# Merge gates and branch projections with the activations held in the array instead of the weights

## The chip, the core and the metric

One core of a Trainium2 chip runs the whole program. The metric is device time in microseconds (us), the median of three runs. TensorE (PE) multiplies, VectorE (DVE) and ScalarE (ACT) do the elementwise work, GpSimd (POOL) a few tiny operations, and SyncE (SP) starts most transfers from memory; ACT starts the others.

## What is computed

One residual block on 256 tokens of 2048 channels: a SwiGLU network, token mixing by three parallel branches, a second SwiGLU network, each between normalizations. The change is in the merge of the branches:

```python
gates = jax.nn.sigmoid(h @ w_merge_gate[l] + b_merge_gate[l])     # 2048 -> 3 x 2048
g_fox, g_diff, g_mem = jnp.split(gates, 3, axis=-1)
merged = (g_fox * (y_fox @ w_branch_fox[l])                       # 1024 -> 2048
          + g_diff * (y_diff @ w_branch_diff[l])                  #  512 -> 2048
          + g_mem * (y_mem @ w_branch_mem[l]))                    #  512 -> 2048
x = x + rmsnorm(merged @ w_out[l], mix_post_g[l])
```

## The kernel before

All weights stream through once, about 430 MB in pieces of 512 KB. SP loads a piece (`raw`, L65, six buffers), ACT rounds it to float32r (`hi`, L90), DVE computes the remainder (`lo`, L91), and TensorE reads both (four buffers of `hi` and `lo`). `Stream.ahead` (L69) issues ACT's and DVE's work for the pieces to come, as far as the four buffers allow, so the work for the piece that is three further on waits until TensorE has finished the piece before the current one. Everything runs in the order in which it is written: each engine, and SP's queue of transfers, takes its instructions in program order.

A product is made of three float32r products, hi*hi, hi*lo and lo*hi, and there are two forms:

- `mm_a` (L203) holds a 128 x 128 block of weights in the array and moves the activations through it, which lie transposed (channels on the partitions): `hi` with 512 columns (256 tokens, their hi and lo parts side by side) and `lo` with 256 columns. The result has channels on the partitions and must be summed from the two halves of its bank (`lr_sum`, L415).
- `mm_b` (L226) holds a 128 x 128 block of activations (128 tokens) and moves 512 columns of weights: three matmuls of 512 columns for each of the two token halves `t`. The result has tokens on the partitions. A piece is 12 such matmuls. Both feed-forward networks, the value projection (428 columns) and the output projection work like this.

The merge (L938 to L974) uses `mm_a`. It loops over 16 groups `m` of 128 output channels: three gate products with `h2T` (the normalized activations) of 16 row blocks each, then 16 row blocks of branch products with `y_a` and `y_b`. For each `m`, ACT and DVE sum the halves, scale by the row `hrow`, add the bias and take the sigmoid (L967, bias by partition from `colt`), multiply, add, and split the sum into `mT` (L974), which is already laid out as the output projection wants it. In the first group the rest of the attention steps runs between the products (`fill`); what is left is drained at once (L947).

The feed-forward networks hold the activations too, and their results must be turned. They do this block by block of 512 channels: DVE transposes 32 x 32 squares (L442) into `fz`; 16 small transfers on SP's queue move the squares to their partitions (`regroup`, L444, into `fw`), issued after the second piece of the next block; after its seventh piece ACT and DVE split the result into the next input (`split`, L451). The tables of offsets `OFF` and `OFF_V` shift operands by 32 and 112 bytes from the start of a 256-byte line. `PostProj` (L359) is the output projection with its normalization; its gain rows `g_row` are 256 KB transfers on ACT's queue (L374), broadcast to all partitions.

Of the kernel before, what the change touches and what calls it, by code (L numbers as in the profile page):

```python
# [16 lines left out]
P = 128  # L17
# [16 lines left out]

C_G1, C_GM, C_GMEM, C_G2, C_B, C_HG = 0, 16, 32, 48, 64, 112
N_COLS = 113


class Stream:
# [29 lines left out]
    def ahead(self, most=8):  # L69

        for _ in range(most):
            if self.done == len(self.plan):
                break
            _, ap, extra = self.plan[self.done]
# [12 lines left out]
            hi, lo = (pool.tile([P, D // 2], F32R, tag=t + tag, name=t, align_bytes=LINE)[:, off:off + 2 * step]  # L87
                      .rearrange("p (k n) -> p k n", k=2)[:, :, 0:w] for t in ("hi", "lo"))
# [22 lines left out]
def tile_block(ctx, tc, x, mem, xt, memt, f1gu, f1d, wqk, wv, wmkv, wgate, wbr, wout, f2gu, f2d,  # L111
# [84 lines left out]

    def rows_of(pool, n, off, **kw):

        t = pool.tile([P, n * 2 * S + OFF], F32R, align_bytes=LINE, **kw)
        return t[:, off:off + n * 2 * S].rearrange("p (k s n) -> p k s n", k=n, s=2)  # L200
# [224 lines left out]
    def times_row(dst, row):  # L425
        if row is not None:
            nc.vector.tensor_tensor(out=dst, in0=dst, in1=row, op=ALU.mult)


    def ffn_up(idx, hT, rstd, setup, groups, inserts):  # L430
# [6 lines left out]
        def product(t, bank):  # L437
# [4 lines left out]
            nc.vector.transpose(out=state["z"][:, t], in_=sg[:, t])  # L442

        def regroup():  # L444

            for a in range(4):
                for q in range(4):
                    nc.sync.dma_start(out=state["w"][32 * q:32 * q + 32, :, a],
                                      in_=state["z"][32 * a:32 * a + 32, :, P * q:P * (q + 1)])

        def split(n):  # L451
            src = state["w"].rearrange("p t a (k i) -> p k (t a) i", k=4)
            hi, lo = (state["gh"][:, 4 * n:4 * n + 4, i].rearrange("p k (g i) -> p k g i", i=32) for i in range(2))
            for k in range(4):
                split_to(hi[:, k], lo[:, k], src[:, k])

# [5 lines left out]
        for n in range(FB):  # L462
# [12 lines left out]
            for t in range(2):  # L475
                product(t, bu[t])
            late = {1: regroup, 6: lambda n=n: split(n)}
        return state["gh"], late
# [6 lines left out]
    tp1 = g1_stack.enter_context(tc.tile_pool(name="ft1", bufs=1, side="left", reuse_waits="tile"))  # L485
    hT1 = rows_of(hpool, KT, 0, name="hT1")
    gh1 = rows_of(gp1, FT, 0, name="gh1")
    zeros = hpool.tile([P, 512], BF16, name="zeros")
# [49 lines left out]
    fgp = fg_stack.enter_context(tc.tile_pool(name="fg1", bufs=1, side="right", reuse_waits="tile"))  # L538
    mha = rows_of(yap, 8, 0, tag="y", name="mha")
    macc = [small.tile([P, 4], F32, name=f"macc{t}", bufs=1) for t in range(2)]  # L540
# [40 lines left out]
    h2T = rows_of(h2p, KT, OFF, tag="h", name="h2T")  # L581
    mhb = rows_of(ybp, 8, 0, tag="y", name="mhb")

# [170 lines left out]

    y_a = rows_of(yap, 8, OFF, tag="y", name="y_a")
    y_b = rows_of(ybp, 8, OFF, tag="y", name="y_b")

# [179 lines left out]

    mg_stack = ExitStack()  # L938
    mT = None
    for m in range(KT):  # L940
        zs = []
        for b in range(3):
            z = zp.tile([P, S], F32, tag="z", name="z", bufs=4)
            lr_sum(z, proj_a("gate", h2T), zp)
            times_row(z, hrow)
            zs.append(z)
        if m == 0:  # L947
            while fill.left():
                fill(drain=True)
            at_stack.close()  # L950
            mgp = mg_stack.enter_context(tc.tile_pool(name="mgp", bufs=1, side="left", reuse_waits="tile"))
            mT = rows_of(mgp, KT, 0, name="mT")
        bb = [new_bank("mm_br") for _ in range(3)]
        lims = [(0, 8), (8, 12), (12, 16)]
        for half in range(2):
            st.ahead()
            w, = st.take("br")
            for kk in range(8):
                k = half * 8 + kk
                i = 0 if k < 8 else (1 if k < 12 else 2)  # L960
                mm_a(bb[i], w, kk, (y_a, y_b)[half], kk, k == lims[i][0], k == lims[i][1] - 1)
            st.release()
        acc = None
        for b in range(3):
# [12 lines left out]


    h3T = rows_of(h2p, KT, 0, tag="h", name="h3T")
    fg_stack = ExitStack()  # L980
# [13 lines left out]

    post2.body()
    banks = post2.last(lag=7, first_done=first_half,
# [6 lines left out]
    def setup2():  # L1003
        fg_stack.close()
        mg_stack.close()
        yb_stack.close()
        gp = g2_stack.enter_context(tc.tile_pool(name="gh2", bufs=1, side="right", reuse_waits="tile"))
        tp = g2_stack.enter_context(tc.tile_pool(name="ft2", bufs=1, side="right", reuse_waits="tile"))
        return tp, rows_of(gp, FT, 0, name="gh2")

# [117 lines left out]
```

## Time and profile before

| | |
|---|---|
| median of three runs | 2212.86 us (2212.7 to 2212.89) |
| the profiled execution's own time | 2212.4 us |
| its span, first to last instruction | 2210.6 us |
| TensorE busy | 2200.3 us, 100% of the span, 10560 matmuls |
| DVE / ACT busy | 1284.7 us (58%) / 1035.8 us (47%) |
| mean granted TensorE clock | 0.999 |
| HBM read | 423.28 MB, 192 GB/s over the span |

A busy time is the time in which an engine has at least one instruction under way. Matmuls overlap each other, so a matmul's own duration (0.39 us for 512 columns) says little; what counts is the distance from one start to the next. The merge runs from about 1020 to 1393 us; the output projection follows until 1481 us.

### The profile page before, as it was taken

What the parts mean: (1) busy time and instruction counts of PE and PEld (TensorE: products, weight loads), DVE (VectorE), ACT (ScalarE), POOL (GpSimd) and SP (SyncE); (2) the same over time, 40 slices, a digit from 0 to 9 for tenths busy, and PEclk for the clock granted to TensorE, in tenths of its full rate; (3) what the DMA queues carried; (4) which work ended last, traced back from release to release, by engine and by line L of the source; (5) the groups of instructions that cost most, each with busy time, mean ns of one, the idle gap of its engine ahead of it and who ended that gap; (6) DMA issues with size and microseconds to landing.
All of it is one profiled execution on the core that took longest, in us unless ns stands there. A gap on an engine that the chain in (4) does not pass through costs nothing. (4 is left out here: it accounts for less than half of the span.)

```text
span 2210.6 us, 28170 instructions
## 1 busy us (share of the span) xinstructions
PE 2200.3 (100%) x10560; PEld 1865.1 (84%) x10560; DVE 1284.7 (58%) x1621; ACT 1035.8 (47%) x1452; POOL 13.5 (1%) x25
## 2 busy tenths in 40 slices
PE   9999999999999999999999999999999999999998
PEld 7888888888888899988888888888888888888887
DVE  6555555555444756766676767566555555554444
ACT  6444444444444644544555555456444444444442
POOL 0000000000000100000000000000000000000000
PEclk9999999999999999999999999999999999999999
DMA  8666656667766564544556565655766666666664
GB/s 307 198 226 208 201 186 231 204 211 231 224 207 198 172 192 150 181 161 150 185 189 191 186 194 186 207 182 173 236 204 199 198 220 205 189 217 213 197 198 131
DMA packets 150840, 438.78 MB, mean 198 GB/s; under 512 B 19632, under 2 KB 42544, under 8 KB 150704
## 3 DMA queue, kind: packets, MB, share of 16 engines
q1 hardware_dynamic: 145088, 427.96, 60.0%
q10 hardware_dynamic: 5616, 9.03, 1.3%
q8 instruction: 82, 1.34, 0.2%
q14 instruction: 54, 0.44, 0.1%
HBM read 423.28 MB, written 2.10 MB: 192 GB/s over the span
## 5 line engine op out<-in xcount | busy, mean ns | idle before, releaser
L91 DVE TENSOR_TENSOR lo<-raw,hi 128x1024 fp32r<-128x1024 f32 (+2 forms) x794 | 957.2, 1211 | 761.4 <-ACT hi L90 736.0
L90 ACT CAST hi<-raw 128x1024 fp32r<-128x1024 f32 (+2 forms) x794 | 818.9, 1037 | 846.2 <-PE mm_b L236 744.8
L207 PE MATMUL mm_a<-h2T,hi 128*128 128x512 f32 x1088 | 384.0, 395 | 0.0
L209 PE MATMUL mm_a<-h2T,lo 128*128 128x256 f32 x1088 | 306.8, 282 | 0.0
L234 PE MATMUL mm_b<-hi,hT 128*128 128x512 f32 x704 | 274.4, 390 | 0.5 <-ACT hi L90 0.5
L234 PE MATMUL mm_b<-hi,h3T 128*128 128x512 f32 x704 | 274.9, 390 | 0.0
L235 PE MATMUL mm_b<-lo,hT 128*128 128x512 f32 x704 | 274.5, 390 | 0.2 <-DVE lo L91 0.2
L236 PE MATMUL mm_b<-hi,h3T 128*128 128x512 f32 x704 | 274.4, 390 | 0.0
L236 PE MATMUL mm_b<-hi,hT 128*128 128x512 f32 x704 | 274.3, 390 | 0.0
L234 PE MATMUL mm_b<-hi,gh 128*128 128x512 f32 x704 | 274.3, 390 | 0.0
L235 PE MATMUL mm_b<-lo,h3T 128*128 128x512 f32 x704 | 274.3, 390 | 0.0
L236 PE MATMUL mm_b<-hi,gh 128*128 128x512 f32 x704 | 274.3, 390 | 0.0
L235 PE MATMUL mm_b<-lo,gh 128*128 128x512 f32 x704 | 274.3, 390 | 0.0
L207 PEld LDWEIGHTS mm_a<-h2T,hi 128*128 128x128 f32 x1088 | 204.5, 188 | 41.5
L209 PEld LDWEIGHTS mm_a<-h2T,lo 128*128 128x128 f32 x1088 | 206.3, 190 | 0.2
L235 PEld LDWEIGHTS mm_b<-lo,hT 128*128 128x128 f32 x704 | 132.2, 188 | 28.2 <-DVE lo L91 0.8
L234 PEld LDWEIGHTS mm_b<-hi,hT 128*128 128x128 f32 x704 | 132.2, 188 | 28.2 <-ACT hi L90 1.0
L236 PEld LDWEIGHTS mm_b<-hi,gh 128*128 128x128 f32 x704 | 132.2, 188 | 27.5
L236 PEld LDWEIGHTS mm_b<-hi,h3T 128*128 128x128 f32 x704 | 132.2, 188 | 27.3
L234 PEld LDWEIGHTS mm_b<-hi,gh 128*128 128x128 f32 x704 | 132.2, 188 | 27.3
L234 PEld LDWEIGHTS mm_b<-hi,h3T 128*128 128x128 f32 x704 | 132.3, 188 | 27.2
L235 PEld LDWEIGHTS mm_b<-lo,gh 128*128 128x128 f32 x704 | 132.2, 188 | 27.2
(208 smaller groups left out, 1940.8 us busy)
## 6 DMA issues: line engine op xcount, KB each, us to landing
raw<-in_f1gu SPq DMA_DIRECT2D x176, 512.0 KB, 5.0
raw<-in_f2gu SPq DMA_DIRECT2D x176, 512.0 KB, 4.8
raw<-in_wgate SPq DMA_DIRECT2D x96, 512.0 KB, 4.3
raw<-in_f1d SPq DMA_DIRECT2D x88, 512.0 KB, 4.5
raw<-in_f2d SPq DMA_DIRECT2D x88, 512.0 KB, 4.2
raw<-in_wv SPq DMA_DIRECT2D x48, 428.0 KB, 3.4
raw<-in_wqk SPq DMA_DIRECT2D x40, 512.0 KB, 4.4
raw<-in_wbr SPq DMA_DIRECT2D x32, 512.0 KB, 4.0
```

The source lines that it names most:

```text
L90: self.nc.scalar.copy(out=hi[:, i], in_=src[:, i])
L91: self.nc.vector.tensor_tensor(out=lo[:, i], in0=src[:, i], in1=hi[:, i].bitcast(F32), op=ALU.subtract)
L207: nc.tensor.matmul(bank, lhsT=hi[:, i, c], rhs=act[:, k].rearrange("p s n -> p (s n)"), start=start, stop=False)
L209: nc.tensor.matmul(bank[:, 0:S], lhsT=lo[:, i, c], rhs=act[:, k, 0], start=False, stop=stop)
L234: nc.tensor.matmul(o, lhsT=xh, rhs=wh, start=start and kk == 0, stop=False)
L235: nc.tensor.matmul(o, lhsT=xh, rhs=wl, start=False, stop=False)
L236: nc.tensor.matmul(o, lhsT=xl, rhs=wh, start=False, stop=stop and kk == 1)
```

## The change

The merge is written with `mm_b`. It loops over four blocks `n` of 512 output channels and, inside, over the three branches: 8 pieces of gate products into two banks, then 4 pieces (first branch) or 2 pieces (second and third) of branch products into two others. DVE scales a gate bank by the token's factor and adds the bias (L966); the bias is now a row of 512 channels, broadcast to all partitions by a 256 KB transfer on ACT's queue that stands in program order behind the gate's last piece (L963). ACT takes the sigmoid, DVE multiplies by the branch bank and adds up in `acc`. The first three blocks are turned as in the feed-forward networks: two DVE transposes, 16 small transfers after the second piece of the next block, the split after its seventh (`turned_block`, the old `regroup` and `split` moved out). The last block is turned by eight TensorE transposes after the second and third piece of the output projection. The weights of the first three blocks are reordered on the host, so that the turned squares come out in place. `y_a`, `y_b` lose their 32-byte shift, the gate weights get it; `h2T` keeps its own. A scratch size drops from 4096 to 2048 bytes, and `cols` loses its 48 bias columns.

```diff
-C_G1, C_GM, C_GMEM, C_G2, C_B, C_HG = 0, 16, 32, 48, 64, 112
+C_G1, C_GM, C_GMEM, C_G2, C_HG = 0, 16, 32, 48, 64
...
-            off, step = (OFF_V, NBS) if w == NB else (0, w)
+            off, step = (OFF_V, NBS) if w == NB else (OFF if name == "gate" else 0, w)
...
-    for m in range(KT):
-        for b in range(3):
-            st.add("gate", wgate[b * KT + m])
-        st.add("br", wbr[m])
+    for n in range(4):
+        for b, (lo, hi) in enumerate(((0, 2), (2, 3), (3, 4))):
+            for i in range(4):
+                st.add("gate", wgate[(4 * b + n) * 4 + i])
+            for i in range(lo, hi):
+                st.add("br", wbr[4 * n + i])
...
+    def turned_block(z, w, dst, n, at=(1, 6)):
+        def regroup():
+            for a in range(4):
+                for q in range(4):
+                    nc.sync.dma_start(out=w[32 * q:32 * q + 32, :, a],
+                                      in_=z[32 * a:32 * a + 32, :, P * q:P * (q + 1)])
+        def split():
+            src = w.rearrange("p t a (k i) -> p k (t a) i", k=4)
+            hi, lo = (dst[:, 4 * n:4 * n + 4, i].rearrange("p k (g i) -> p k g i", i=32) for i in range(2))
+            for k in range(4):
+                split_to(hi[:, k], lo[:, k], src[:, k])
+        return {at[0]: regroup, at[1]: split}
...
-    y_a = rows_of(yap, 8, OFF, tag="y", name="y_a")
-    y_b = rows_of(ybp, 8, OFF, tag="y", name="y_b")
+    y_a = rows_of(yap, 8, tag="y", name="y_a")
+    y_b = rows_of(ybp, 8, tag="y", name="y_b")
...
+    late = {}
+    for n in range(4):
         acc = None
-        for b in range(3):
-            g = zs[b]
-            c = C_B + b * KT + m
-            nc.scalar.activation(out=g, in_=g, func=AF.Sigmoid, bias=colt[:, c:c + 1])
-            br = zp.tile([P, S], F32, tag="br", name="br")
-            lr_sum(br, bb[b], zp)
-            nc.vector.tensor_tensor(out=g, in0=br, in1=g, op=ALU.mult)
-            if acc is not None:
-                nc.vector.tensor_tensor(out=g, in0=acc, in1=g, op=ALU.add)
-            acc = g
-        split_to(mT[:, m, 0], mT[:, m, 1], acc)
+        for b, y in enumerate((y_a, y_b[:, 0:4], y_b[:, 4:8])):
+            banks = proj_b("gate", h2T, KT, 512, steps=late)
+            late = {}
...
+            bias = mwp.tile([P, 512], F32, tag="bias", name="bias", bufs=2)
+            nc.scalar.dma_start(out=bias, in_=rows[3 + b:4 + b, 512 * n:512 * (n + 1)].partition_broadcast(P)[:, 0])
+            g = mwp.tile([P, 2, 512], F32, tag="g", name="g", bufs=2)
+            for t in range(2):
+                nc.vector.scalar_tensor_tensor(out=g[:, t], in0=banks[t], scalar=hr[t], in1=bias,
+                                               op0=ALU.mult, op1=ALU.add)
+                nc.scalar.activation(out=g[:, t], in_=g[:, t], func=AF.Sigmoid)
+            banks = proj_b("br", y, 8 if b == 0 else 4, 512)
...
+            for t in range(2):
+                o = acc[:, t] if b == 0 else g[:, t]
+                nc.vector.tensor_tensor(out=o, in0=banks[t], in1=g[:, t], op=ALU.mult)
+                if b:
+                    nc.vector.tensor_tensor(out=acc[:, t], in0=acc[:, t], in1=g[:, t], op=ALU.add)
+        if n < 3:
+            for t in range(2):
+                nc.vector.transpose(out=z[:, t], in_=acc[:, t])
+            late = turned_block(z, w, mT, n)
...
+    def last_block(t):
+        tr = trp.tile([P, 4, P], F32, tag="tr", name="tr_z")
+        for k in range(4):
+            nc.tensor.transpose(tr[:, k], acc[:, t, P * k:P * (k + 1)], ident)
+        split_to(*(mT[:, 12:16, i, t * P:(t + 1) * P] for i in range(2)), tr)
+    late = {1: lambda: last_block(0), 2: lambda: last_block(1)}
...
-    post2.body()
+    post2.body(late)
```

How the order of the instructions moves is seen at three places. The first is TensorE at the step from a gate product to a branch product (the third group `m` before, the first block's second branch now). Before:

```order
L209 MATMUL mm_a<-h2T,lo 128x256
L207 MATMUL mm_a<-h2T,hi 128x512
L209 MATMUL mm_a<-h2T,lo 128x256
L207 MATMUL mm_br<-y_a,hi 128x512
L209 MATMUL mm_br<-y_a,lo 128x256
L207 MATMUL mm_br<-y_a,hi 128x512
```

Now:

```order
L236 MATMUL mm_b<-hi,h2T 128x512
L237 MATMUL mm_b<-lo,h2T 128x512
L238 MATMUL mm_b<-hi,h2T 128x512
L236 MATMUL mm_b<-hi,y_b 128x512
L237 MATMUL mm_b<-lo,y_b 128x512
L238 MATMUL mm_b<-hi,y_b 128x512
```

Matmuls of 512 and 256 columns in turn became matmuls of 512 columns throughout.

The second is ACT, in the group `m` = 1 before:

```order
L90 CAST hi<-raw 128x1024 x2
L967 ACTIVATE z<-z,colt 128x256
L418 ACTIVATE left<-mm_br 128x256
L967 ACTIVATE z<-z,colt 128x256
L418 ACTIVATE left<-mm_br 128x256
L967 ACTIVATE z<-z,colt 128x256
L418 ACTIVATE left<-mm_br 128x256
L290 CAST mT<-z 128x256
```

and now, from the last gate of the first block to the first gate of the second:

```order
L963 DMA bias<-in_rows 128x512
L968 ACTIVATE g<-g 128x512 x2
L90 CAST hi<-raw 128x1024 x9
L292 CAST mT<-mw 128x256 x4
L90 CAST hi<-raw 128x1024
L963 DMA bias<-in_rows 128x512
L968 ACTIVATE g<-g 128x512 x2
```

Behind the four casts that wait for the small transfers stand one more weight cast, the start of the bias transfer, and the two sigmoids, which wait for DVE, which waits for the bias.

The third is SP's queue at the same place. Before, it holds weight loads only:

```order
L65 DMA raw<-in_wgate 128x1024 x6
L65 DMA raw<-in_wbr 128x1024 x2
L65 DMA raw<-in_wgate 128x1024 x6
L65 DMA raw<-in_wbr 128x1024 x2
L65 DMA raw<-in_wgate 128x1024 x6
```

and now:

```order
L65 DMA raw<-in_wgate 128x1024 x8
L65 DMA raw<-in_wbr 128x1024 x3
L438 DMA mw<-mz 32x2x128 x16
L65 DMA raw<-in_wbr 128x1024
L65 DMA raw<-in_wgate 128x1024 x8
```

The 16 small transfers (`mw` from `mz`) stand between the third and the fourth load of branch weights for the next block.

## Rows read from the trace of the kernel before

**Rows 1.** The page: busy time by engine.

```profile
PE 2200.3 (100%) x10560; PEld 1865.1 (84%) x10560; DVE 1284.7 (58%) x1621; ACT 1035.8 (47%) x1452; POOL 13.5 (1%) x25
```

**Rows 2.** Windows, merge: stretch, length, busy PE, PEld, DVE, ACT, POOL; clock, DMA share, GB/s.

```profile
1020.00:1031.00 11.00, 11.00 (x68) 9.70 (x67) 7.06 (x14) 4.34 (x11) 0.00 (x0) 1.00 0.47 142
1031.00:1392.90 361.90, 361.90 (x2095) 321.55 (x2094) 254.28 (x379) 188.68 (x300) 0.00 (x0) 1.00 0.59 187
```

**Rows 3.** Timeline of PE, merge: first gate matmuls of groups 1 and 3.

```profile
1060.26 0.39 PE L207 MATMUL mm_a<-h2T,hi 128*128 128x512 f32 x1
...
1104.63 0.39 PE L207 MATMUL mm_a<-h2T,hi 128*128 128x512 f32 x1
```

**Rows 4.** Timeline of PE, output projection: two matmuls 15 apart.

```profile
1420.28 0.39 PE L234 MATMUL mm_b<-hi,mT 128*128 128x512 f32 x1
...
1423.68 0.39 PE L234 MATMUL mm_b<-hi,mT 128*128 128x512 f32 x1
```

**Rows 5.** Timeline of PE, value projection (428 columns): two matmuls 56 apart.

```profile
799.69 0.36 PE L235 MATMUL mm_b<-lo,h2T 128*128 128x428 f32 x1
...
810.51 0.36 PE L234 MATMUL mm_b<-hi,h2T 128*128 128x428 f32 x1
```

**Rows 6.** Timeline of PE, second network: a group of four transposes between matmuls.

```profile
1496.66 0.40 PE L236 MATMUL mm_b<-hi,h3T 128*128 128x512 f32 x1
1496.89 0.60 PE L328 MATMUL tr_h<-ident,x_sb 128*128 128x128 f32 x4
1497.24 0.48 PE L234 MATMUL mm_b<-hi,h3T 128*128 128x512 f32 x1
1497.56 0.40 PE L235 MATMUL mm_b<-lo,h3T 128*128 128x512 f32 x1
```

**Rows 7.** Timeline of DVE, second network, end of a block.

```profile
1615.02 0.74 DVE L440 SCALAR_TENSOR_TENSOR fs<-mm_b,rstd_tok,fs 128x512 f32<-128x512 f32 x1
...
1617.18 0.71 DVE L442 STREAM_TRANSPOSE fz<-fs 128x512 f32<-128x512 f32 x1
...
1619.32 1.23 DVE L91 TENSOR_TENSOR lo<-raw,hi 128x1024 fp32r<-128x1024 f32 x1 [0.32 <-ACT hi L90]
```

**Rows 8.** Timeline of SP's queue, the same block: its small transfers.

```profile
1620.95 11.45 SPq L448 DMA_DIRECT2D fw<-fz  x16
```

**Rows 9.** Timeline of ACT, the same block: split, weight cast, activation.

```profile
1633.74 1.33 ACT L290 CAST gh<-fw 128x256 fp32r<-128x256 f32 x4 [0.86 <-DMA fw<-fz]
1634.98 1.04 ACT L90 CAST hi<-raw 128x1024 fp32r<-128x1024 f32 x1
...
1637.28 0.69 ACT L435 ACTIVATE fs<-mm_b,rstd_tok 128x512 f32<-128x512 f32 x1 [0.67 <-PE mm_b L236]
```

**Rows 10.** Timeline of ACT and its queue, end of the merge.

```profile
1396.02 0.41 ACT L290 CAST mT<-z 128x256 fp32r<-128x256 f32 x1 [2.37 <-DVE z L972]
1396.02 0.33 ACTq L374 DMA_DIRECT2D g_row<-in_rows  x1
```

**Rows 11.** All 12 transfers of gain rows: issue, and time to landing.

```profile
L374 ACTq DMA_DIRECT2D g_row<-in_rows x12: 334/334/335, 486.0 to 2144.1; - x12
...
DMA to landing us min/median/max: 3.1/3.9/6.1
```

**Rows 12.** Windows behind the quickest (1396.0) and slowest (1459.7) of them; behind rows 8.

```profile
1396.00:1399.00 3.00, 3.00 (x15) 2.47 (x14) 1.94 (x3) 2.66 (x4) 0.00 (x0) 1.00 0.25 87
1460.00:1466.00 6.00, 6.00 (x28) 4.99 (x27) 2.76 (x5) 2.33 (x4) 0.00 (x0) 1.00 0.99 371
1636.00:1639.00 3.00, 3.00 (x15) 2.50 (x14) 1.29 (x2) 2.23 (x4) 0.00 (x0) 1.00 1.02 356
```

**Rows 13.** Tile `raw` on SP's queue, two weight loads issued 1634.1 to 1634.6: landing.

```profile
DMA to landing us min/median/max: 7.6/8.0/8.4
```

**Rows 14.** Groups by line and shape, DVE: a product from a bank, a sum in SBUF.

```profile
L378 DVE TENSOR_TENSOR fg<-mm_b,g_row 128x512 f32<-128x512 f32 x24 | 15.6, 682 | 0.0
...
L339 DVE TENSOR_TENSOR h3T<-tg,h3T 128x512 fp32r<-128x512 f32 x7 | 4.8, 692 | 0.2
```

More of the change, by code (lines that the diff above doesn't have):

```diff
@@ L33 @@
 OFF_V = 28
[L35 to L36 removed]
+C_G1, C_GM, C_GMEM, C_G2, C_HG = 0, 16, 32, 48, 64
+N_COLS = 65
 class Stream:
@@ L73, in ahead @@
                 break
-            _, ap, extra = self.plan[self.done]
+            name, ap, extra = self.plan[self.done]
             if extra:
@@ L442, in product @@
             nc.vector.transpose(out=state["z"][:, t], in_=sg[:, t])
[L444 to L455, printed above, removed]
         def open_block():
@@ L476, in ffn_up @@
                 product(t, bu[t])
-            late = {1: regroup, 6: lambda n=n: split(n)}
+            late = turned_block(state["z"], state["w"], state["gh"], n)
         return state["gh"], late
@@ L935, in tile_block @@
             fill.add(mem_unit(h // 2, head("mq", sc)), 2)
[L938 to L941, printed above, removed]
-        for b in range(3):
[L943 to L962, printed above, removed]
-        acc = None
-        for b in range(3):
-            g = zs[b]
-            c = C_B + b * KT + m
-            nc.scalar.activation(out=g, in_=g, func=AF.Sigmoid, bias=colt[:, c:c + 1])
-            br = zp.tile([P, S], F32, tag="br", name="br")
-            lr_sum(br, bb[b], zp)
-            nc.vector.tensor_tensor(out=g, in0=br, in1=g, op=ALU.mult)
-            if acc is not None:
-                nc.vector.tensor_tensor(out=g, in0=acc, in1=g, op=ALU.add)
-            acc = g
-        split_to(mT[:, m, 0], mT[:, m, 1], acc)
@@ new lines, in tile_block @@
+    mg_stack, mw_stack = ExitStack(), ExitStack()
+    late = {}
+    for n in range(4):
+        acc = None
+        for b, y in enumerate((y_a, y_b[:, 0:4], y_b[:, 4:8])):
+            banks = proj_b("gate", h2T, KT, 512, steps=late)
+            late = {}
+            if n == b == 0:
+                while fill.left():
+                    fill(drain=True)
+                at_stack.close()
+                mgp = mg_stack.enter_context(tc.tile_pool(name="mgp", bufs=1, side="left", reuse_waits="tile"))
+                mT = rows_of(mgp, KT, name="mT")
+                z = mgp.tile([P, 2, 512], F32, name="mz")
+                w = mgp.tile([P, 2, 4, P], F32, name="mw")
+                mwp = mw_stack.enter_context(tc.tile_pool(name="mwp", bufs=1, side="left", reuse_waits="tile"))
+            bias = mwp.tile([P, 512], F32, tag="bias", name="bias", bufs=2)
[6 more added lines that the diff above has]
+            banks = proj_b("br", y, 8 if b == 0 else 4, 512)
+            if acc is None:
+                acc = mgp.tile([P, 2, 512], F32, tag="acc", name="acc", bufs=1)
+            for t in range(2):
[7 more added lines that the diff above has]
+            late = turned_block(z, w, mT, n)
@@ L1078, with turned @@
     cols = np.concatenate([col(W["ffn1_pre_g"]), col(W["mix_pre_g"]), col(W["mem_norm_g"]), col(W["ffn2_pre_g"]),
-                           col(W["b_merge_gate"]), col(W["diff_head_g"])], axis=1)
-    rows = np.stack([W["ffn1_post_g"], W["mix_post_g"], W["ffn2_post_g"]])
+                           col(W["diff_head_g"])], axis=1)
+    def turned(v):
+        v = v.reshape(-1, D)
+        return np.concatenate([v[:, :D - 512].reshape(-1, 3, 4, 4, 32).transpose(0, 1, 3, 2, 4).reshape(-1, D - 512),
+                               v[:, D - 512:]], axis=1)
+    rows = np.concatenate([np.stack([W["ffn1_post_g"], W["mix_post_g"], W["ffn2_post_g"]]),
+                           turned(W["b_merge_gate"])])
     lamv = np.stack([W["diff_lambda_q1"], W["diff_lambda_k1"], W["diff_lambda_q2"], W["diff_lambda_k2"]])
@@ L1107 @@
         "wmkv": _tiles_b(np.concatenate([W["w_mem_kv"][:, 512:], W["w_mem_kv"][:, :512]], axis=1), 512),
-        "wgate": _tiles_a(W["w_merge_gate"]),
-        "wbr": _tiles_a(np.concatenate([W["w_branch_fox"], W["w_branch_diff"], W["w_branch_mem"]], axis=0)),
+        "wgate": _tiles_b(np.concatenate([turned(v) for v in np.split(W["w_merge_gate"], 3, axis=1)], axis=1), 512),
+        "wbr": _tiles_b(turned(np.concatenate([W["w_branch_fox"], W["w_branch_diff"], W["w_branch_mem"]], axis=0)), 512),
         "wout": _tiles_b(W["w_out"], 512),
```

21 lines of the change are left out of this document (11 added, 10 removed).

## The prediction

> **What bounds the kernel now.** I read the page first: TensorE is busy for 2200.3 of 2210.6 us [rows 1]. Then the windows of the merge: in its 361.9 us TensorE is busy all of it, while DVE has 254 us of work and ACT 189 [rows 2]. So nobody is waited for there, and less work on DVE or ACT gives nothing by itself. What the change can win is TensorE's own time for the same products; what it can lose is the cover: a piece of weights that comes later than TensorE wants it. Then I read distances between starts, since the durations overlap, and last the nearest copy of the new code, the turned blocks of the feed-forward network.
>
> **The products.** The merge has 16 groups of (3 x 16 + 16) = 64 row blocks, 1024 pairs of `mm_a`. Groups 1 and 3 start 44.37 us apart, which is 128 pairs: 346.64 ns a pair [rows 3], 355.0 us for 1024. The new form has 4 x (24 + 8) = 128 pieces of 12 matmuls, 1536 in all. Fifteen such matmuls take 3.40 us in the output projection, 226.7 ns each [rows 4], so 348.2 us. **-6.8 us.** Columns alone cost 213.3 ns for 512 at 2.4 GHz (the granted clock is 1.00 in all windows), and 320 for the 768 of a pair; so each matmul has 13.3 ns on top in both forms, and the win is the 512 matmuls that vanish.
>
> The Trainium skill ("TensorE: Matmul & The Clock Gate", Back-to-back issue gap) gives an isolated matmul 2.5 ns on top of its columns. By that the 512 matmuls would be worth 1.3 us and not 6.8. The trace disagrees with it in both forms.
>
> Will the operand placement keep the 13.3? `h2T` stays shifted by 32 bytes and is now the operand held in the array, with weights shifted by 32; no row shows that pair. Unshifted on both sides gives 13.3 [rows 4]; `h2T` held with weights at 112 bytes gives 10.82 us for 56 matmuls of 428 columns, 193.2 ns or 14.9 on top [rows 5]. I take 13.3, the placement with no difference between the two operands; at 14.9 the 1152 gate matmuls would cost 1.8 us more. Nothing in the trace has less than 13.3, in either form, so I take that as the floor.
>
> **The last block.** Two groups of four transposes are added to TensorE. Such a group takes 0.58 instead of 0.23 us to the next matmul, and that one 0.32 instead of 0.23 to its successor [rows 6]: 0.44 each, **+0.9 us**. Their results are covered: `acc` is complete four DVE operations (2.7 us) after the last product, the transposes come after 5.4 us (two pieces), the split ends before 12 us, and the first output product that needs it is piece 6, at 16.3 us. Without that cover a late split would stop TensorE one for one.
>
> **The first block's attention steps.** Two steps that were drained together now run one by one; the extra change between kinds of matmul costs about what the last line of the group in rows 6 shows, **+0.1**.
>
> **DVE, ACT, the transfers.** Removed are the sums of halves, the row scaling and 16 splits; added are 24 scalings, 24 sigmoids, 40 products and sums of 0.68 to 0.69 us [rows 14], 6 transposes, 12 small splits. All that is below the old load. Twelve bias transfers and 48 small ones add little to a DMA share of 0.59 [rows 2]. The narrower `cols` and the smaller scratch I cost at nothing: the one is covered at the start by the first piece of weights, which ACT needs too, and no transfer of this program is started by POOL, so nothing asks for the other.
>
> **The waits.** This is where I expect something back. Call E the end of a gate's 8 pieces (21.8 us). In the stretch after E, DVE must have the bias, then: two scalings (0.74 each), the second sigmoid (0.69, as the Silu in rows 9), the next `hi` (1.04), its `lo` (1.23). With the small overlaps of DVE's and ACT's starts I add 4.4 us from the landing of the bias to that `lo` [rows 7, 9]. TensorE wants it three pieces after E, at E+8.2, and the `lo` one matmul later: E+8.4. So the bias may land until **E+4.0** without a wait.
>
> In eight of the twelve gates (second and third branch) ACT reaches the bias right behind a weight cast that starts 2.7 us before E; a transfer starts together with the operation ahead of it, as [rows 10] shows for a gain row. Landing takes 3.1 to 6.1 us [rows 11], so at the latest E+3.6: no wait. In the very first gate the transfer stands behind the last attention step, at E+0.1; at a DMA share of 0.47 [rows 2] and 4 us it lands at E+4.1: **+0.1**.
>
> The three others are the first gates of blocks 2, 3 and 4, where ACT has the four split casts ahead of it. In the network, DVE's work on a block starts at 1615.0, the second `lo` ends at 1620.55, SP starts the 16 small transfers at 1620.95, and ACT's casts start 12.8 us after that, at 1633.74, having waited for them [rows 7 to 9]. There the casts come 3.0 us before E. In the merge the block's end is later: the last branch product ends 5.4 us after its gate. From the gate's end, DVE has two scalings (bias landed at +1.3), two `lo`, two products and two sums (0.68, 0.69), two transposes and two `lo`: done 8.2 us after the block's end instead of 5.5. The small transfers start at 8.6 and the casts at 21.2 to 21.4, which is E-0.5. Then come 1.33 us of casts and the `hi` cast. The bias starts between E-0.6 (if ACT's queue passes it while the casts run) and E+0.8 (with the start of `hi`). Rows 10 are nearest to the first; I take E-0.4.
>
> How long does it take to land? After the small transfers SP fetches the loads it is behind with, and the DMA share is 1.02 [rows 12]. At a share of 0.25 a gain row took 3.1 us, at 0.99 it took 6.1 [rows 11, 12]. I take 5.5, near the busy end. The bias lands at E+5.1, the `lo` is there at E+9.5, and TensorE waits 1.1 us; three times, **+3.3 us**. The bounds are nothing (a landing within 4.4) and 2.9 each, 8.7 in all (E+0.8 and 6.1). What is queued behind the waiting scaling on DVE are the next `lo`s; they catch up at 1.2 us per 2.7 us piece.
>
> The Trainium skill ("DMA: Bandwidth & Descriptors", Queues, rings and completion order) says that each DMA engine takes turns between the queues, a packet at a time, so that ACT's transfer would not stand behind all of SP's loads. By that rule there would be next to no wait, which is the first rival; the gain row that took 6.1 us with such loads beside it speaks against it.
>
> **Sum**, against the profiled execution's own 2212.4: -6.8 + 0.9 + 0.1 + 0.1 + 3.3 = -2.4, so 2210.0. The median of the runs is 0.46 higher, so I say **2210.5**.
>
> **Rivals.** (1) *The bias lands in time.* One load of 512 KB at the 371 GB/s of the busy stretch [rows 12] takes 1.4 us; if a bias waits for just one, it lands 3.1 + 1.4 = 4.5 after its start, at E+4.1, and hardly anything is lost. Then it is 2212.86 - 6.8 + 0.9 + 0.2 = **2207.1**. For it: the median landing of 3.9 [rows 11]. Against it: the 6.1 [rows 12].
> (2) *The bias is as late as the loads beside it.* Loads issued behind the small transfers took 7.6 to 8.4 us [rows 13]. With 8.0 the bias lands at E+7.6, TensorE waits 3.6 us in each of three blocks, 10.8 in all: 2212.86 - 5.8 + 10.8 = **2217.9**, slower than before. It decides from a landing of 7.8 us on. Against it: no gain row took more than 6.1.
> (3) *Vanished matmuls are worth nothing, and only columns count.* Both forms move 786,432 columns (1024 x 768, 1536 x 512), so the 6.8 us would not come: 2212.86 + 0.9 + 0.2 + 3.3 = **2217.3**. Against it stand the 13.3 ns in rows 3 and 4, the same for 256 and 512 columns taken together as for 512 alone. The Trainium skill's isolated gap ("TensorE: Matmul & The Clock Gate", Back-to-back issue gap) would bring the kernel near to this.
>
> **How the numbers follow.** The forecast with its own spread (waits of 1.5 to 8.7 us in all) has 0.60, rival 1 0.30, rival 2 0.08, rival 3 0.02. About 0.2%, or 4.4 us, is what a measurement of this kernel can tell from no change. Rival 1 is below 2208.4; rivals 2 and 3 are at or above 2217.3: faster 0.30, same 0.60, slower 0.10. The range starts just below rival 1, at 2206.9, and ends at 2215.0, which takes in most of the bounds of the waits and leaves rivals 2 and 3 out.
>
> **What would show it.** Right: 1536 matmuls `mm_b` at 0.227 us between starts; no idle TensorE inside a gate; three gaps of about 1 us, each in the first branch product of blocks 2, 3 and 4, ended by DVE's `lo`, with DVE having waited for the bias; two groups of transposes at 0.44. Rival 1: no such gaps, bias landings below 4.5 us. Rival 2: gaps of over 3 us. The forecast is wrong in its base if the distance between gate matmuls is not 0.227, or if gaps stand elsewhere, at the second and third branches or in the output projection.

## The result and the profile after

The changed kernel takes 2226.46 us (2225.38 to 2228.77, five runs) against 2212.89 us of the kernel before in the same session; the ratio is 1.0063 with a 95% interval of 1.0052 to 1.0074. It is slower by 13.6 us, outside the range of 2206.9 to 2215.0. The profiled execution took 2227.11 us, 14.7 more than that of before. TensorE has 504 matmuls fewer, and yet it is busy for longer; the mean granted clock fell from 0.999 to 0.996.

The page of the changed kernel, busy time by engine, beside [rows 1]:

```profile
PE 2204.5 (99%) x10056; PEld 1841.5 (83%) x10056; DVE 1239.3 (56%) x1465; ACT 1001.0 (45%) x1330; POOL 13.5 (1%) x25
```

Where the time went is quickest seen from the start of the first matmul of each stage (us). The fourth column is the version of the first experiment below, which has the change without its waits.

| start of | before | after | after, bias early |
|---|---|---|---|
| the first down product | 485.80 | 487.09 | 486.73 |
| the output projection (`mT`) | 1393.06 | 1406.77 | 1388.01 |
| the second network (`h3T`) | 1481.04 | 1495.77 | 1477.01 |
| the last matmul on `gh` in the first group of `mm_b` (L234 before, L236 after) | 2202.2 | 2216.9 | 2198.1 |

The start lost 1.3 us, the stages from there to the output projection 12.4, the output projection 1.0, and nothing after that. In the second of these stretches, this is what TensorE waited for in the merge (waits of PE, 1020 to 1410 us: who waited for whom, total us, times, longest):

```profile
PE mm_b L236 <- ACT hi L90: 8.3, 3, 3.4
PE mm_b L237 <- DVE lo L91: 2.1, 4, 0.8
```

Three waits for a `hi`, each followed by one for the `lo`: once in each of the blocks 2, 3 and 4, in the fourth piece of the first branch product, where the prediction had put them. (The fourth wait for a `lo`, 0.2 us, lies in the first branch product of block 1.) The chain behind the first of them goes through ACT and its queue (timeline of ACT, start, duration, operation; in brackets the idle time before it and what ended it):

```profile
1143.63 1.05 ACT L90 CAST hi<-raw 128x1024 fp32r<-128x1024 f32 x1 [1.67 <-PE mm_b L238]
1148.26 0.41 ACT L292 CAST mT<-mw 128x256 fp32r<-128x256 f32 x1 [3.58 <-DMA mw<-mz]
1148.43 0.37 ACTq L963 DMA_DIRECT2D bias<-in_rows  x1
1148.57 1.02 ACT L292 CAST mT<-mw 128x256 fp32r<-128x256 f32 x3
1149.49 1.04 ACT L90 CAST hi<-raw 128x1024 fp32r<-128x1024 f32 x1
1158.34 1.29 ACT L968 ACTIVATE g<-g 128x512 f32<-128x512 f32 x2 [7.80 <-DVE g L966]
1159.54 3.87 ACT L90 CAST hi<-raw 128x1024 fp32r<-128x1024 f32 x4
```

and through DVE (timeline of DVE, the same stretch):

```profile
1157.56 1.41 DVE L966 SCALAR_TENSOR_TENSOR g<-mm_b,rstd_tok,bias 128x512 f32<-128x512 f32 x2 [5.76 <-DMA bias<-in_rows]
1160.60 4.63 DVE L91 TENSOR_TENSOR lo<-raw,hi 128x1024 fp32r<-128x1024 f32 x4 [1.63 <-ACT hi L90]
```

The gate ends at E = 1148.88 here, the start of the first `y_a` matmul. The split casts start at E-0.6, the bias transfer at E-0.4 while they run. Then nothing happens on ACT or DVE until the bias lands 9.0 us later; the `hi` that TensorE wants at E+8.2 starts only at E+10.7. In the other two blocks the transfer starts 0.4 and 0.2 us before E and takes 8.1 and 7.7 us. Why so long? SP's queue shows it (timeline of SP):

```profile
1136.31 10.57 SPq L438 DMA_DIRECT2D mw<-mz  x16
1146.98 0.53 SPq L65 DMA_DIRECT2D raw<-in_wbr  x1
1147.61 16.84 SPq L65 DMA_DIRECT2D raw<-in_wgate  x8
```

For 10.6 us SP starts only small transfers while TensorE uses up four pieces. Then five loads of 512 KB follow in 2.1 us, three of them before the bias and two right behind it. Those five (tile `raw`, 1146.9 to 1149.1) and the bias (tile `bias`, 1148 to 1149) took:

```profile
DMA to landing us min/median/max: 4.8/7.7/9.8
```

```profile
DMA to landing us min/median/max: 9.0/9.0/9.0
```

So the bias is as late as the loads beside it. What was moved in that time, by queue (q1 is SP's, q10 ACT's; packets, MB, share of the 16 DMA engines), from 1148.4 to 1153.0 and from there to 1157.5:

```profile
q1 hardware_dynamic: 335, 1.25, 89.4%
```

```profile
q1 hardware_dynamic: 422, 1.54, 85.7%
q10 hardware_dynamic: 144, 0.26, 16.6%
```

In the first 4.6 us after its start no packet of the bias moves. SP's queue moves 1.25 MB, four fifths of the three loads that had been started ahead (1.22 and 1.23 MB in the same 4.6 us of blocks 3 and 4). Only then do both queues move at once. The third part is on TensorE itself (timeline of PE):

```profile
1156.83 0.39 PE L238 MATMUL mm_b<-hi,y_a 128*128 128x512 f32 x1
1160.62 0.79 PE L236 MATMUL mm_b<-hi,y_a 128*128 128x512 f32 x1 [3.39 <-ACT hi L90]
1161.87 0.79 PE L237 MATMUL mm_b<-lo,y_a 128*128 128x512 f32 x1 [0.47 <-DVE lo L91]
1162.47 0.63 PE L238 MATMUL mm_b<-hi,y_a 128*128 128x512 f32 x1
1162.89 0.63 PE L236 MATMUL mm_b<-hi,y_a 128*128 128x512 f32 x1
1163.32 0.63 PE L237 MATMUL mm_b<-lo,y_a 128*128 128x512 f32 x1
...
1167.53 0.40 PE L238 MATMUL mm_b<-hi,h2T 128*128 128x512 f32 x1
```

Behind the stall the matmuls are 0.427 us apart instead of 0.227 (512 columns at 1.2 GHz are 0.427). The windows before, in and behind it say the same in the clock column, the seventh number of a row (after length and the busy times):

```profile
1148.40:1157.06 8.66, 8.66 (x39) 6.94 (x37) 2.66 (x5) 2.14 (x5) 0.00 (x0) 1.00 0.96 332
1157.06:1162.47 5.41, 1.55 (x4) 0.79 (x4) 3.29 (x4) 4.10 (x6) 0.00 (x0) 0.83 0.23 95
1162.47:1167.50 5.03, 5.03 (x13) 3.96 (x12) 3.88 (x5) 1.46 (x2) 0.00 (x0) 0.51 0.84 253
1167.50:1180.00 12.50, 12.50 (x56) 10.32 (x55) 5.79 (x6) 4.71 (x5) 0.00 (x0) 1.00 0.67 213
```

From 1156.83 to 1167.53 there are 15 steps, 3.40 us at the usual distance, and 10.70 passed: 7.3 us lost. Of these 4.6 are the stall (3.56 until the `hi` matmul, 1.02 more until the `lo` matmul), and 2.7 the lower clock. Blocks 3 and 4, counted the same way, lost 5.5 (3.75 and 1.7) and 5.2 (3.5 and 1.7). In all 18.0 us, 11.9 of them stall and 6.2 clock.

### The profile page after: what moved, and what is told of

It reads as the page before. It is cut to its first block, busy times and chain, and to the rows that moved or that the text cites. A ratio compares the mean times of both kernels' runs of the same rounds, so it can differ in the third digit from the quotient of the medians.

```text
span 2225.3 us, 26910 instructions
## 1 busy us (share of the span) xinstructions
PE 2204.5 (99%) x10056; PEld 1841.5 (83%) x10056; DVE 1239.3 (56%) x1465; ACT 1001.0 (45%) x1330; POOL 13.5 (1%) x25
## 5 line engine op out<-in xcount | busy, mean ns | idle before, releaser
L236 PE MATMUL mm_b<-hi,hT 128*128 128x512 f32 x704 | 274.3, 390 | 0.4 <-ACT hi L90 0.4
L236 PE MATMUL mm_b<-hi,h3T 128*128 128x512 f32 x704 | 274.4, 390 | 0.0
L236 PE MATMUL mm_b<-hi,gh 128*128 128x512 f32 x704 | 273.9, 389 | 0.0
L236 PE MATMUL mm_b<-hi,h2T 128*128 128x512 f32 (+1 forms) x576 | 220.5, 383 | 0.0
L237 PE MATMUL mm_b<-lo,h2T 128*128 128x512 f32 (+1 forms) x576 | 217.9, 378 | 0.3 <-DVE lo L91 0.3
L238 PE MATMUL mm_b<-hi,h2T 128*128 128x512 f32 (+1 forms) x576 | 217.7, 378 | 0.0
L236 PEld LDWEIGHTS mm_b<-hi,hT 128*128 128x128 f32 x704 | 132.2, 188 | 29.1 <-ACT hi L90 1.7
L236 PEld LDWEIGHTS mm_b<-hi,gh 128*128 128x128 f32 x704 | 132.1, 188 | 27.5
L238 PEld LDWEIGHTS mm_b<-hi,hT 128*128 128x128 f32 x704 | 132.1, 188 | 27.4
L236 PEld LDWEIGHTS mm_b<-hi,h3T 128*128 128x128 f32 x704 | 132.1, 188 | 27.3
```

The costliest lines, as they stand in the source:

```text
L236: nc.tensor.matmul(o, lhsT=xh, rhs=wh, start=start and kk == 0, stop=False)
L237: nc.tensor.matmul(o, lhsT=xh, rhs=wl, start=False, stop=False)
L238: nc.tensor.matmul(o, lhsT=xl, rhs=wh, start=False, stop=stop and kk == 1)
```

## The experiments

Theory A: the whole loss comes from the bias of the first gates of blocks 2 to 4, which stands behind the split casts in ACT's queue and so starts when SP has just thrown its backlog of loads onto the DMA engines; the stall it causes costs its length and then the clock. Theory B: the split casts themselves, which wait for the small transfers, hold ACT's weight casts up. Theory C: the broadcast is slow in this stretch wherever it is started.

**Bias early.**

In the cuts of code of this section `...` stands for what is left out; `load_bias(n, b, queue)` holds the two lines of the old transfer.

```diff
+            if n or b:
+                bias = load_bias(n, b, nc.scalar)
             banks = proj_b("gate", h2T, KT, 512, steps=late)
...
-            bias = mwp.tile([P, 512], F32, tag="bias", name="bias", bufs=2)
-            nc.scalar.dma_start(out=bias, in_=rows[3 + b:4 + b, ...].partition_broadcast(P)[:, 0])
+            if n == b == 0:
+                bias = load_bias(n, b, nc.scalar)
```

> Eleven of the twelve bias transfers are started before the gate's eight pieces instead of behind them (the very first stays). Theory A: the whole loss comes from the late bias of the first gates of blocks 2 to 4 (three waits of 3.5 to 4.6 us, and matmuls at granted clock 0.50 after each). Then the three gaps go, TensorE's clock stays at 1.00 through the merge, and the time falls by the 18.1 us that I count in the three places: 2208.4 us (2207.5 to 2209.5), faster than the kernel before by 0.2%. Theory B: the split casts, which wait for the 16 small transfers, hold ACT's weight casts up by themselves, and the bias only came last. Then gaps of 1 us or more stay in the first branch of blocks 2 to 4, ended by ACT's casts, and the time is 2214 or more.

2208.43 us (2208.1 to 2208.68), 0.998 of before (0.9971 to 0.9989). The window over the whole merge of this version shows no idle TensorE and no fall of the clock:

```profile
1020.00:1410.00 390.00, 390.00 (x1754) 323.05 (x1753) 230.51 (x254) 170.23 (x198) 0.00 (x0) 1.00 0.63 201
```

The three losses vanish in full (2226.46 - 2208.43 = 18.0, as counted). The split casts still wait for the small transfers, but with every bias early these begin earlier too, and the casts start at E-3.3, E-2.8 and E-3.3. So this run alone does not clear them; theory B is decided by the run below that moves the bias ahead of them. This version is faster than both kernels, than the one before by 0.2%.

**Bias on SP's queue, right behind the small transfers.**

```diff
+            def moves_and_bias(n=n, moves=moves):
+                nonlocal bias
+                moves()
+                bias = load_bias(n + 1, 0, nc.sync)
...
+            late[1] = moves_and_bias
```

> Only the three late bias transfers move: SP starts them right behind the 16 small transfers and ahead of the nine weight loads, some 1.5 us before the changed kernel's ACT does. Theory A (the bias is slow because nine loads of 512 KB were started before it and fill the DMA engines): it lands in 3 to 4 us, about 1.5 us behind the gate's end, nobody waits, 2208.5 us (2207.5 to 2210). Theory C (a broadcast to 128 partitions is slow in this stretch wherever it is started): it lands after 8 to 9 us as now, 6.6 us behind the gate's end, TensorE still waits some 2.6 us per block plus the time at the lower clock: 2218 to 2222.

2209.29 us (2208.25 to 2210.11), 0.9984 of before (0.9975 to 0.9993). The timeline of SP in block 2 of this version, and the landing of the transfer in its second row (tile `bias`, 1144 to 1146):

```profile
1134.22 10.76 SPq L438 DMA_DIRECT2D mw<-mz  x16
1145.08 0.53 SPq L948 DMA_DIRECT2D bias<-in_rows  x1
1145.71 0.38 SPq L65 DMA_DIRECT2D raw<-in_wbr  x1
```

```profile
DMA to landing us min/median/max: 5.9/5.9/5.9
```

It starts at E-2.95 and lands at E+2.95, so nobody waits; theory C falls. In the changed kernel three loads, and not nine, had been started before the bias, as SP's queue showed above. My 3 to 4 us for the landing were too few: 5.9, 4.6 and 5.0 in the three blocks. Loads that start right behind a transfer seem to slow it too, only less than those ahead of it; no run changes that alone.

**Bias on ACT's queue, ahead of the split casts instead of behind them.**

```diff
+            def bias_and_split(n=n, split=split):
+                nonlocal bias
+                bias = load_bias(n + 1, 0, nc.scalar)
+                split()
...
+            late[6] = bias_and_split
```

> Of the changed kernel, only the three late bias transfers move, and only by four casts: ACT starts them right ahead of the split casts instead of behind them and the weight cast. ACT has then nothing else to do for 3.6 us, so they start some 4 us before the gate's end, while the small transfers still run and before the weight loads. Theory A: landing in 4 to 6 us, 0 to 2 us behind the gate's end, no wait: 2208.5 us (2208.1 to 2209.5). Rival (the loads that follow 2 us later slow it as much as those ahead of it): 8 to 9 us, 4 to 5 behind the gate's end, waits of up to 1 us a block: 2210.5 to 2212.

2208.38 us (2207.89 to 2209.45), 0.998 of before (0.9971 to 0.999). Timeline of ACT, block 2, and the landing of that transfer:

```profile
1143.08 1.05 ACT L90 CAST hi<-raw 128x1024 fp32r<-128x1024 f32 x1 [1.67 <-PE mm_b L238]
1143.08 0.34 ACTq L948 DMA_DIRECT2D bias<-in_rows  x1
1147.23 1.33 ACT L292 CAST mT<-mw 128x256 fp32r<-128x256 f32 x4 [3.11 <-DMA mw<-mz]
```

```profile
DMA to landing us min/median/max: 3.4/3.4/3.4
```

The same transfer on the same queue, five operations earlier in the program and some 5 us earlier in time, lands in 3.4 us instead of 9.0. It starts while SP still starts small transfers, so these do not slow it, and 2.5 us ahead of the first load (1145.62); its packets move from 1.0 us after its start on. The split casts start at E-1.1, E-0.4 and E-1.0 here, near E-0.6, E-0.6 and E-0.4 of the changed kernel, and TensorE waits for nothing in the merge: theory B falls. One place in the order of ACT's queue is worth 18 us.

**All blocks turned by TensorE.** No small transfers, no casts that wait for them; the bias stays behind the gate.

```diff
-            for t in range(2):
-                nc.vector.transpose(out=z[:, t], in_=acc[:, t])
-            late = turned_block(z, w, mT, n)
+            late = {3: lambda n=n, a=acc: turn(n, 0, a), 4: lambda n=n, a=acc: turn(n, 1, a)}
...
```

> All four blocks are turned by TensorE (transposes behind the fourth and fifth piece of the next gate), so there are no small transfers, no casts that wait for them and no weights reordered; the bias stays where the change has it, behind the gate. Theory A: the bias then starts 2.7 us before the gate's end with no backlog of loads, lands in 4 to 5.2 us as in the other gates, no gaps; six more groups of transposes cost 0.44 each: 2208.4 + 2.6 = 2211.0 us (2210 to 2212.5). Theory C (late wherever it starts in these gates): gaps stay, 2220 or more.

2211.28 us (2211.03 to 2211.86), 0.9993 of before (0.9984 to 1.0002). Landings of the bias are 3.9 to 5.5 us, TensorE waits for nothing in the merge. Without casts that wait and without the backlog, the bias behind the gate starts 2.5 us before the gate's end and is early enough, and the turning by small transfers is worth 2.9 us over that by TensorE (2211.28 - 2208.43; 2.6 expected).

**The stall filled.** The bias stays late; TensorE multiplies for nothing meanwhile.

```diff
+            def busy():
+                bank = trp.tile([P, 512], F32, tag="tr", name="busy")
+                for _ in range(18):
+                    nc.tensor.matmul(bank, lhsT=y_a[:, 0, 0, 0:P], rhs=y_a[:, 0]..., start=True, stop=True)
-            banks = proj_b("br", y, 8 if b == 0 else 4, 512)
+            banks = proj_b("br", y, 8 if b == 0 else 4, 512, steps={2: busy} if n and b == 0 else {})
```

> The bias stays late; 18 matmuls of 512 columns whose result nobody reads are added on TensorE behind the third piece of the first branch product of blocks 2 to 4, where it stands still (18 x 0.227 = 4.1 us against stalls of 4.6, 3.75 and about 3.7). Theory A, with the clock as a cost of its own: the waits stay (they are only filled), but the granted clock stays at 1.00 behind them and the 6.2 us at the lower level are not lost: 2220.5 us (2219 to 2222). Rival: what follows the gap is slow because the next lo pieces come late, not because of the clock. Then the matmuls behind the filling are spaced by DVE's lo, and the time is 2226 to 2228.

2221.97 us (2221.28 to 2222.66), 1.0041 of before (1.0026 to 1.0057), so 4.5 less than the changed kernel though it does more. Timeline of PE, block 2:

```profile
1156.10 4.24 PE L972 MATMUL busy<-y_a 128*128 128x512 f32 x18
1160.18 0.39 PE L236 MATMUL mm_b<-hi,y_a 128*128 128x512 f32 x1
1160.63 0.50 PE L237 MATMUL mm_b<-lo,y_a 128*128 128x512 f32 x1
1160.97 0.39 PE L238 MATMUL mm_b<-hi,y_a 128*128 128x512 f32 x1
1161.20 0.39 PE L236 MATMUL mm_b<-hi,y_a 128*128 128x512 f32 x1
```

The same late bias, and the matmuls behind it are 0.23 apart, not 0.43: the slowness behind the stall was the clock, not the supply of `lo`. That 4.5 came back and not 6.2 is because the three fillings took 13.6 us, 12.2 of them matmuls and 1.4 what was left of the waits, in place of stalls of 11.9.

**Stalls of chosen length.** On the version with the bias early, ACT gets extra casts ahead of the weight cast in question (five in the first run, seven in the second).

```diff
+            for _ in range(5 if n and b == 0 else 0):
+                nc.scalar.copy(out=z..., in_=h2T[:, 0:2]...)
             banks = proj_b("br", y, 8 if b == 0 else 4, 512)
```

> The version with early bias transfers; ACT gets five extra casts of 128x1024 (about 0.98 us each, result unread) ahead of the weight cast of the fourth branch piece in blocks 2 to 4. In the version without them DVE ends that piece's lo 4.0 us before TensorE wants it, so the lo comes 0.9 us late: three short stalls, near the 1.1 us of the forecast. If a stall costs its length only: 2208.4 + 2.7 = 2211.1 us (2210.3 to 2212), clock 1.00. If TensorE's clock falls behind a stall as short as that, as it did behind those of 3.7 us, 1.5 us more per block: 2214 to 2216.

2213.55 us (2212.98 to 2215.9), 1.0005 of before (0.9996 to 1.0014). An extra cast took 1.06 us and not 0.98, so the `lo` came 1.4 to 2.2 us late (1.7, 2.2 and 1.4, from the starts as above), three stalls of 5.3 together; 2208.43 + 5.3 = 2213.7, near the median, which lies between my two ranges. The rows of PE in its blocks 2 and 3:

```profile
1157.24 0.50 PE L236 MATMUL mm_b<-hi,y_a 128*128 128x512 f32 x1 [0.54 <-ACT hi L90]
1158.50 0.50 PE L237 MATMUL mm_b<-lo,y_a 128*128 128x512 f32 x1 [0.76 <-DVE lo L91]
...
1246.83 0.50 PE L236 MATMUL mm_b<-hi,y_a 128*128 128x512 f32 x1 [1.02 <-ACT hi L90]
1248.09 0.51 PE L237 MATMUL mm_b<-lo,y_a 128*128 128x512 f32 x1 [0.76 <-DVE lo L91]
1248.42 0.60 PE L238 MATMUL mm_b<-hi,y_a 128*128 128x512 f32 x1
1248.83 0.63 PE L236 MATMUL mm_b<-hi,y_a 128*128 128x512 f32 x1
```

Behind the stall of block 2 (and that of block 4) the clock stayed; behind that of block 3 it fell. The profiled execution, with one fall, is the longest of the ten runs (2215.9 us). By the median, then, stalls not much longer than those that I had forecast mostly cost their length and nothing more; the clock of the other nine runs was not seen stall by stall.

> The same with seven extra casts: the lo comes 2.9 us late in each of the three blocks (hi about 1.9 us). At its length alone: 2208.4 + 8.7 = 2217.1 us. With the clock falling behind each stall as in the changed kernel (1.5 us each by the run with filled stalls): 2221.7. I expect the second, 2220 to 2223, and the granted clock at 0.50 for some 2 to 4 us behind each stall.

2225.31 us (2225.13 to 2227.73), 1.006 of before (1.0045 to 1.0075). Three stalls of 11.1 us together (3.8, 3.8 and 3.5, where I had 2.9 each, so that the time is above my range), and 16.9 us lost (2225.31 - 2208.43): 5.8 at the lower clock. With bias transfers that are early, this rebuilds most of the 18.0 us of the changed kernel. The stall makes the loss, whatever its cause.

**Gate weights not shifted.** On the version with the bias early.

```diff
-            off, step = (OFF_V, NBS) if w == NB else (OFF if name == "gate" else 0, w)
+            off, step = (OFF_V, NBS) if w == NB else (0, w)
```

> The version with early bias transfers, with the gate weights not shifted by 32 bytes (h2T stays shifted). Theory: the 13.3 ns that a matmul has on top grow where the two operands lie differently in their 256-byte lines, as in the value projection (14.9 ns): 1152 gate matmuls, up to 1.8 us more, 2209 to 2210.3. Rival: the shift makes no difference, 2208.4 (2207.9 to 2208.9).

2214.87 us (2214.66 to 2216.32), 1.001 of before (1.0001 to 1.0019): 6.4 us more, over three times my bound. Timeline of PE, two gate matmuls 35 steps apart, 0.2334 us each, 20.1 ns on top of the columns:

```profile
1109.65 0.40 PE L236 MATMUL mm_b<-hi,h2T 128*128 128x512 f32 x1
...
1117.82 0.40 PE L238 MATMUL mm_b<-hi,h2T 128*128 128x512 f32 x1
```

**Nothing shifted.**

```diff
-OFF = 8
+OFF = 0
```

> The version with early bias transfers, with neither h2T nor the gate weights shifted (both begin at the start of a 256-byte line). Theory: only a difference between the operands costs (h2T at 32 bytes against gate weights at 0 took 20 ns on top instead of 13.3). Then gate matmuls are 0.227 us apart as with both shifted; the query and key products, where h2T moves past weights, lose the shift that they have now, and may cost up to 640 x 6.5 ns = 4.2 us more: 2208.4 to 2212.6. Rival: h2T held in the array is slow or fast by its own place; then the gate's distance stays at 0.233 and the time is 2214.9 or more.

2211.08 us (2210.61 to 2211.32), 0.9992 of before (0.9983 to 1.0001). Two gate matmuls 36 steps apart in this version:

```profile
1109.73 0.39 PE L236 MATMUL mm_b<-hi,h2T 128*128 128x512 f32 x1
...
1117.89 0.39 PE L236 MATMUL mm_b<-hi,h2T 128*128 128x512 f32 x1
```

0.2267 again. For the gate it is the difference between the two operands that costs. The 2.7 us on top of the version with the bias early come only in part from the query and key products, where I had expected them: there a pair takes 0.353 us over twelve pairs (904.68 to 908.92) where the shifted `h2T` gives 0.347, and that stretch, up to the first gate matmul, is 1.5 us longer (899.89 to 1036.80 against 898.18 to 1033.62). More comes from the value projection, which I had left out: it is 2.0 us longer (772.98 to 899.89 against 773.30 to 898.18). Two of its matmuls 56 apart in this version, to be set beside [rows 5]:

```profile
799.72 0.36 PE L237 MATMUL mm_b<-lo,h2T 128*128 128x428 f32 x1
...
810.92 0.36 PE L236 MATMUL mm_b<-hi,h2T 128*128 128x428 f32 x1
```

That is 0.2000 us each, 21.7 ns on top of the columns, with `h2T` held at the start of a line and weights at 112 bytes; with `h2T` at 32 bytes it was 14.9. The merge is 0.6 us shorter and the start 0.3 earlier.

**The start.** All versions of the change begin the first down product 0.6 to 1.3 us later than the 485.8 of before.

```diff
-C_G1, C_GM, C_GMEM, C_G2, C_HG = 0, 16, 32, 48, 64
-N_COLS = 65
+C_G1, C_GM, C_GMEM, C_G2, C_HG = 0, 16, 32, 48, 112
+N_COLS = 113
...
```

> The version with early bias transfers, with the 48 unused bias columns put back into cols (113 columns as before the change). All four versions with 65 columns begin the first down product 0.6 to 1.3 us later than the kernel before. Theory: with fewer columns that transfer lands 0.45 us sooner, ACT's first operation and SP's third x transfer move up with it, ahead of weight loads, and the second weight piece lands later; then the first down product starts at 485.8 us again and the time is 2207.7 (2207.2 to 2208.1). Rival: the start differs from run to run by that much; then 2208.4 (2208.1 to 2208.7).

2208.97 us (2208.52 to 2209.79), 0.9983 of before (0.9974 to 0.9991), first down product at 487.1: the narrower `cols` are not the reason.

```diff
-    nc = bacc.Bacc(..., dynamic_dma_scratch_size=4096)
+    nc = bacc.Bacc(..., dynamic_dma_scratch_size=2048)
```

> The kernel before, with nothing changed but the scratch size, 2048 bytes instead of 4096. All versions with 2048 begin the first down product 0.6 to 1.3 us later than the one profile of before. If the scratch does that, this kernel begins it at 486.4 to 487.1 and takes 2213.4 us (2213.2 to 2213.8); if not, 485.8 and 2212.8 (2212.5 to 2213.1).

2212.72 us (2212.49 to 2213.13), 0.9999 of before (0.999 to 1.0008), first down product at 486.0: nor is the scratch.

> The kernel before once more, for a second profile of its start. If the start differs from run to run, the first down product begins anywhere from 485.8 to 487.1 us; if it belongs to the kernel, at 485.8 again. Time 2212.8 us.

2212.53 us, first down product at 485.8 again. So the late start belongs to the changed program. It is there from the second piece of weights on, whose first cast starts at 8.40 us instead of 7.12. What makes that piece land later stays open; the order of the arrays in memory was not tried.

## Why the prediction was wrong, step by step

- **The products, -6.8.** Right in mechanism, and 0.227 us per matmul to the digit: eighteen steps from 1116.16 to 1120.24 in a gate of the changed kernel. From the first gate matmul to the output projection the version without waits takes 354.4 us (1033.62 to 1388.01) where the kernel before took 360.1 (1032.95 to 1393.06): -5.7. The missing 1.1 us were mostly not in the sum: a block takes 87.24 us from one first branch product to the next (1148.10 to 1235.34) and not the 384 x 0.2267 = 87.05 that I had, 0.2 a block at the six changes of operand; the rest lies with the attention steps of the first block, which cost 0.3 where I had 0.1. Rival 3 falls: vanished matmuls were worth about what rows 3 and 4 said. That the trace disagrees with a gap of 2.5 ns holds for these float32r products only: in the attention step, three bf16 matmuls of 128 columns start 0.05 to 0.06 us apart (1036.04, 1036.10, 1036.15), close to the 0.053 of the columns alone.
- **The shift.** I took 13.3 ns and bounded it by 14.9. The choice was right; the bound was for another thing, as the value projection has both operands shifted, by 32 and 112 bytes. The gate with one operand shifted and one not has 20.1.
- **The last block, +0.9.** Measured 0.44 a group: the matmul behind it follows after 0.35 us and its successor after 0.32, as in [rows 6]. The output projection took 1.0 more.

```profile
1412.22 0.60 PE L987 MATMUL tr_z<-ident,acc 128*128 128x128 f32 x4
1412.57 0.48 PE L236 MATMUL mm_b<-hi,mT 128*128 128x512 f32 x1
1412.89 0.40 PE L237 MATMUL mm_b<-lo,mT 128*128 128x512 f32 x1
```

- **Where the casts and the bias start.** Casts at E-0.5 (measured -0.6, -0.6, -0.4), bias at E-0.4 (measured -0.4, -0.4, -0.2), 4.4 us from the landing to the `lo` (4.4 in all three blocks), TensorE's demand at E+8.4. This chain, taken from the turned blocks of the feed-forward network, held to 0.2 us. In the very first gate the bias started at E+0.4 instead of E+0.1, and 0.4 us were lost there instead of 0.1.
- **How long the bias takes to land: the step that failed.** "I take 5.5, near the busy end"; it took 9.0, 8.1 and 7.7 us. By the prediction's own chain that alone turns 1.1 us per block into 4.6, 3.7 and 3.3, and 4.6, 3.75 and 3.5 were measured. I priced it by its kind, the gain rows [rows 11], and took the slowest of twelve as near the end. The nearer row was in my own list: the loads issued behind the small transfers of the feed-forward network took 7.6 to 8.4 us [rows 13], and this transfer starts in just such a place. Rival 2 had the mechanism, with 3.6 us a block, and got 0.08, with "no gain row took more than 6.1" against it, which is again the kind and not the place. The Trainium skill ("DMA: Bandwidth & Descriptors", Queues, rings and completion order) says that a DMA engine takes turns between the queues. I had read from it that ACT's transfer would hardly feel SP's loads. The runs disagree with that reading: 9.0 us behind three loads and ahead of two, 5.9 just ahead of the loads, 3.4 when started 2.5 us ahead of them. The trace of the changed kernel has both queues moving at once, but only from 4.6 us after the transfer's start on, with most of the three loads ahead of it moved; why not sooner, no run shows.
- **A stall costs its length.** The sum had the stalls at their length only. 6.2 us of the 18.0 are matmuls at a granted clock of 0.50 behind them. For the short stalls that I forecast this omission would have been small (the run with five casts); for those that came it was a third of the loss.
- **The start, at nothing.** 0.6 to 1.3 us in the profiles. The two parts that I had named, `cols` and the scratch, do cost nothing; something else does.

The profiled execution: -5.7 for the merge, +18.0 for the three places, +0.4 for the first gate, +1.0 for the output projection, +1.3 at the start and -0.3 between the first down product and the merge are the 14.7 that were measured.

## What to carry to other kernels

Price a transfer by what else is started in the same few us, not by its kind elsewhere: behind a queue that has just caught up on its loads, 256 KB took 7.7 to 9.0 us, and started ahead of that burst 3.2 to 3.4. A transfer whose data is known long before belongs ahead of any instruction on its queue that can wait; here moving it past five casts turned 13.6 us of loss into 4.5 us of gain. Where TensorE is the bound, count a stall of several us at one and a half times its length (18.0 for 11.9 here, 16.9 for 11.1 with seven casts). When operands change roles, measure their places in the 256-byte line anew: the gate wants both at the same place, the query and key products do not.

## What the runs showed of the hardware that I had not expected

- A matmul of 512 columns is 0.2267 us behind the last when both operands begin 32 bytes into a line or both at its start, and 0.2334 when the held one is shifted and the moving one is not: 6.4 us over the merge. Against weights at 112 bytes, in the value projection, `h2T` held at 32 bytes has 14.9 ns on top of its columns and at 0 bytes 21.7. Where `h2T` moves past unshifted weights, in the query and key products, the shift is the better place: 0.347 us a pair, unshifted 0.353. The runs show no rule behind these three.
- TensorE's granted clock fell to 0.50 (1.2 GHz) behind all six stalls of 3.5 to 4.6 us in the profiles, for 1.7 to 2.7 us of loss each in the changed kernel, and behind one of three stalls of 1.4 to 2.2 us. With matmuls that nobody needs in the stall it stayed at 1.00.
